# Four staging units of 12 KB, six output buffers and two turns of loads and stores in a batched matmul

## The chip, the cores and the metric

One core of one Trainium2 chip runs the kernel; the other cores are idle. The metric is the device time in microseconds of one execution. The 51 runs of the kernel before lie between 260.3 and 260.8 us (0.2%). A ratio is the mean time of one kernel's runs over the mean of the other's of the same rounds on the same chip, so it is not quite the ratio of the medians quoted beside it; the run that the profiler took stands among the times, but not in the ratio.

## The reference

```python
batch, m, k, n = 16, 512, 768, 1024
x: (16, 768, 512) float32      y: (16, 768, 1024) float32
out = np.einsum('bkm,bkn->bmn', x, y).astype(np.float32)
```

For each batch 1.57 MB of x and 3.15 MB of y are read and 2.10 MB of output is written: 75.5 MB in, 33.55 MB out.

## The kernel before

SyncE (SP) issues all transfers on one queue. VectorE (DVE) casts float32 to bfloat16, TensorE (PE) multiplies, ScalarE (ACT) copies PSUM to an output buffer. The parts that the change touches (cuts marked):

```python
x_v = x.rearrange("b (p ko) m -> b p ko m", ko=KT)     # KT = 6: a partition holds six rows of K,
y_v = y.rearrange("b (p ko) n -> b p ko n", ko=KT)     # x 12 KB, y 24 KB in one piece
FIRST = 8; TURN = 4; NO = 5
xs = [... sbuf_tensor(f"xs{i}", [P, KT, M], FP32) for i in range(2)]
ys = [... sbuf_tensor(f"ys{i}", [P, KT, N], FP32) for i in range(2)]
ob = [... sbuf_tensor(f"ob{i}", [P, MT, N], FP32) for i in range(NO)]
# ...
def load(b):
    i = b % 2
    if b >= 2:
        nc.sync.wait_ge(cast, nx[b - 2])                # x of b-2 is cast
    wide_dma("x", xs[i][:], x_v[b], 4, True).then_inc(sx[i], 16)
    if b >= 2:
        nc.sync.wait_ge(cast, nx[b - 2] + parts(b - 2)) # y of b-2 is cast
    wide_dma("y", ys[i][:], y_v[b], 2, True).then_inc(sy[i], 16)

for b in range(B):                                      # 8 loads, 4 stores, 4 loads, 4 stores, 4 loads
    load(b)
    if b + 1 >= FIRST and (b + 1 - FIRST) % TURN == 0:
        a = b + 1 - FIRST
        for c in range(a, a + TURN):
            store(c)                                    # waits until batch c + 1 is multiplied
for b in range(B - FIRST + TURN, B - 1):                # 7 stores; the last one follows at the very end
    store(b)
```

`wide_dma` describes a load so that the source is read in packets of 48 KB, four partitions of x or two of y (1440 packets of 49152 B in the trace); only the first load of each kind is described partition by partition (128 packets of 12288 B, 128 of 24576).

Of the kernel before, what the change touches and what calls it, by code (L numbers as in the profile page):

```python
# [3 lines left out]

# [2 lines left out]

# [7 lines left out]
@with_exitstack  # L15
def kernel(
    ctx: ExitStack,
    tc: tile.TileContext,
    x: bass.AP,
    y: bass.AP,  # L20
    out: bass.AP,
):
    nc = tc.nc
    P = 128
    FP32 = mybir.dt.float32
    BF16 = mybir.dt.bfloat16

    B, K, M = x.shape
    _, _, N = y.shape
    KT = K // P  # L30
    MT = M // P
    NF = 512
    NT = N // NF



    x_v = x.rearrange("b (p ko) m -> b p ko m", ko=KT)
    y_v = y.rearrange("b (p ko) n -> b p ko n", ko=KT)
    o_v = out.rearrange("b (p mo) n -> b p mo n", mo=MT)

    FIRST = 8
    TURN = 4
    NO = 5
    KH = KT // 2

    section = ExitStack()
    section.enter_context(tc.tile_critical())
    ec = ctx.enter_context
    xs = [ec(nc.sbuf_tensor(f"xs{i}", [P, KT, M], FP32)) for i in range(2)]
    ys = [ec(nc.sbuf_tensor(f"ys{i}", [P, KT, N], FP32)) for i in range(2)]  # L50
    xb = ec(nc.sbuf_tensor("xb", [P, 2, KT, M], BF16))
    yb = ec(nc.sbuf_tensor("yb", [P, 2, KT, N], BF16))
    ob = [ec(nc.sbuf_tensor(f"ob{i}", [P, MT, N], FP32)) for i in range(NO)]

    HB = MT // 2
    ps = [ec(nc.psum_tensor(f"ps{i}", [P, HB, NT, NF], FP32)) for i in range(2)]
    sx = [ec(nc.semaphore(f"sx{i}")) for i in range(2)]
    sy = [ec(nc.semaphore(f"sy{i}")) for i in range(2)]
    so = [ec(nc.semaphore(f"so{i}")) for i in range(NO)]
    cast = ec(nc.semaphore("cast"))  # L60
    ready = ec(nc.semaphore("ready"))
    room = ec(nc.semaphore("room"))
    groups = ec(nc.semaphore("groups"))
    idle = ec(nc.semaphore("idle"))
    outs = ec(nc.semaphore("outs"))


    made = {}

    def wide_dma(key, dst, src, dram_rows, load):  # L70


        if key not in made:
            made[key] = nc.sync.dma_start(dst, src)
            return made[key]
        pat = mybir.BassSymbolicTensorAccessPattern
        widen = lambda a: a.rearrange("(q r) k m -> q (r k m)", r=dram_rows)
        plain = lambda a: a.rearrange("p k m -> p (k m)")
        s, d = (widen(src), plain(dst)) if load else (plain(src), widen(dst))
        return nc.sync.add_instruction(_copy.replace(  # L80
            made[key].ins, name=nc.get_next_instruction_name(),
            ins=(pat(ap=s.ap, dtype=s.dtype, bass_ap=s, is_dma=False),),
            outs=(pat(ap=d.ap, dtype=d.dtype, bass_ap=d, is_dma=False),),
            sync_info=None, ant_dge_precooked=False))


    def parts(b):
        return 2 if b in (15,) else 1


    nx = [sum(1 + parts(a) for a in range(b)) + 1 for b in range(B)]



    def store(b):


        if b < B - 2:
            nc.sync.wait_ge(groups, 2 * (b + 2))
        else:  # L100
            nc.sync.wait_ge(outs, b - (B - 3))
        nc.sync.dma_start(o_v[b], ob[b % NO][:]).then_inc(so[b % NO], 16)

    def load(b):
        i = b % 2
        if b >= 2:
            nc.sync.wait_ge(cast, nx[b - 2])
        wide_dma("x", xs[i][:], x_v[b], 4, True).then_inc(sx[i], 16)
        if b >= 2:
            nc.sync.wait_ge(cast, nx[b - 2] + parts(b - 2))  # L110
        wide_dma("y", ys[i][:], y_v[b], 2, True).then_inc(sy[i], 16)

    for b in range(B):
        load(b)
        if b + 1 >= FIRST and (b + 1 - FIRST) % TURN == 0:
            a = b + 1 - FIRST
            for c in range(a, a + TURN):
                store(c)
    for b in range(B - FIRST + TURN, B - 1):
        store(b)  # L120


    for _ in range(60):
        nc.vector.sem_inc(idle, 1)
    for b in range(B):
        i = b % 2
        n = 16 * (b // 2 + 1)
        if b >= 2:
            nc.vector.wait_ge(groups, 2 * (b - 1))
        nc.vector.wait_ge(sx[i], n)  # L130
        nc.vector.tensor_copy(xb[:, i], xs[i][:]).then_inc(cast, 1)  # L131
        nc.vector.wait_ge(sy[i], n)
        for h in range(parts(b)):
            ks = slice(h * KT // parts(b), (h + 1) * KT // parts(b))
            nc.vector.tensor_copy(yb[:, i, ks], ys[i][:, ks]).then_inc(cast, 1)  # L135


    for b in range(B):
        nc.gpsimd.wait_ge(cast, nx[b]).then_inc(ready, 1)
        for h in range(parts(b)):  # L140
            nc.gpsimd.wait_ge(cast, nx[b] + h + 1).then_inc(ready, 2 // parts(b))


    x_w = xb[:].rearrange("p s k (j mo) -> p s k mo j", mo=MT)
    pe = OrderedEngineSet([nc.tensor.engine])
    with nc.Fori(0, B // 2, engines=pe):
        with nc.Fori(0, 2, engines=pe) as s:
            nc.tensor.wait_ge(ready, 2).then_inc(ready, -2)
            for mo in range(MT):
                g, m = divmod(mo, HB)  # L150
                if m == 0:
                    nc.tensor.wait_ge(room, 1).then_inc(room, -1)  # L152
                for kt in range(KT):
                    if mo == 0 and kt == KH:
                        nc.tensor.wait_ge(ready, 1).then_inc(ready, -1)
                    for nt in range(NT):
                        mm = nc.tensor.matmul(  # L157
                            ps[g][:, m, nt], x_w[:, bass.ds(s, 1), kt, mo],
                            yb[:, bass.ds(s, 1), kt, nt * NF:(nt + 1) * NF],
                            start=(kt == 0), stop=(kt == KT - 1))  # L160
                if m == HB - 1:
                    mm.then_inc(groups, 1)


    nc.scalar.nop().then_inc(room, 2)
    for _ in range(60):
        nc.scalar.sem_inc(idle, 1)
    for b in range(B):
        if b >= NO:
            nc.scalar.wait_ge(so[b % NO], 16 * (b // NO))  # L170
        for g in range(2):
            nc.scalar.wait_ge(groups, 2 * b + g + 1)
            cp = nc.scalar.copy(ob[b % NO][:, g * HB:(g + 1) * HB].rearrange("p m (t f) -> p m t f", f=NF),  # L173
                                ps[g][:])
            if b < B - 1:
                cp.then_inc(room, 1)
        if b == B - 2:
            nc.scalar.drain().then_inc(outs, 1)
    cp.then_inc(outs, 1)

    for b in range(B - NO, B - 2):
        nc.sync.wait_ge(so[b % NO], 16 * (b // NO + 1))
    section.close()




    nc.sync.dma_start(o_v[B - 1], ob[(B - 1) % NO][:])
# [30 lines left out]
```

## Time and profile before

| | before |
|---|---|
| time, median of 3 runs | 260.7 us (260.4 to 260.74) |
| span of the profile | 258.8 us |
| DMA queue, share of 16 engines | 98.6% |
| PE, DVE, ACT busy | 70%, 32%, 24% |
| transfers | 48 (16 of x, 16 of y, 16 of the output) |

The profile is to be read from the DMA row (the busy share of the sixteen DMA engines in 40 equal slices of the span, in tenths): it is at 8 or 9 in every slice but the first and the last, and every hole of PE lies over a full DMA row. The lines for that are in the prediction. The steady pace of the loads can be read from the casts of y in the timeline (start in us, duration, engine, line, what; in brackets the idle time before it and what ended it):

```profile
36.97 3.36 DVE L135 CAST yb<-ys 128x6144 bf16<-128x6144 f32 x1 [3.58 <-DMA ys<-in_y_dram]
47.97 3.36 DVE L135 CAST yb<-ys 128x6144 bf16<-128x6144 f32 x1 [4.23 <-DMA ys<-in_y_dram]
58.97 3.36 DVE L135 CAST yb<-ys 128x6144 bf16<-128x6144 f32 x1 [4.86 <-DMA ys<-in_y_dram]
```

A batch every 11.00 us, each cast waiting for its data. And the DMA part of the page has a second queue, which it names instruction:

```profile
q14 instruction: 2, 0.02, 0.0%
```

Two blocks of it within the span, at 9 and 11 us.

### The profile page before, as it was taken

The page shows a single profiled execution, that of the slowest core. Times are in us where ns is not written, and L with a number is a line of the kernel's source. Part 1 is how long each engine was busy: PE and PEld are TensorE (multiplying, and loading weights), DVE is VectorE, ACT ScalarE, POOL GpSimd, SP SyncE. Part 2 cuts the span into 40 slices and gives each one's busy share as a digit, 9 for nine tenths or more (in the row PEclk, how much of TensorE's full clock was granted, in tenths as well). Part 3 has the DMA queues.
Part 4 walks back from the last instruction along what each step waited for, and adds up shares of the span by engine and source line. Part 5 has one row for each costly group of instructions (what it writes and reads, how often), then busy time and mean ns, then how long its engine had stood idle before and what let it go on. Part 6 is the DMA issues. An engine that isn't in the chain of part 4 may idle for free. (4 is left out here: it accounts for less than half of the span.)

```text
span 258.8 us, 2506 instructions
## 1 busy us (share of the span) xinstructions
PE 181.6 (70%) x768; PEld 89.3 (34%) x768; DVE 82.0 (32%) x33; ACT 60.9 (24%) x33; POOL 0.2 (0%) x4
## 2 busy tenths in 40 slices
PE   0009999999999006999499920899669980099950
PEld 0004555554545002454145500355325530035520
DVE  0261645527164350011734525002255262300000
ACT  1000442234220005222214002324402200413430
POOL 0000000000000000000000000000000000000000
PEclk9999999999999855899779985699979995569995
DMA  7999989899999999999999989999899999999987
GB/s 273 424 475 410 471 380 479 372 479 395 456 410 441 387 418 430 466 446 418 433 433 425 471 352 443 420 461 479 372 479 403 448 410 390 433 438 420 436 357 324
DMA packets 4514, 109.07 MB, mean 421 GB/s; under 512 B 768, under 2 KB 768, under 8 KB 768
## 3 DMA queue, kind: packets, MB, share of 16 engines
q1 hardware_dynamic: 4512, 109.05, 98.6%
q14 instruction: 2, 0.02, 0.0%
HBM read 75.50 MB, written 33.55 MB: 421 GB/s over the span
## 5 line engine op out<-in xcount | busy, mean ns | idle before, releaser
L157 PE MATMUL ps<-yb,xb 128*128 x768 | 181.6, 402 | 68.0 <-PEq L152 68.0
L157 PEld LDWEIGHTS ps<-yb,xb 128*128 x768 | 89.3, 116 | 159.8 <-issue 89.8
L173 ACT COPY ob<-ps 128x2048 f32<-128x2048 f32 x32 | 59.6, 1872 | 185.3 <-PE ps L157 125.2
L135 DVE CAST yb<-ys 128x6144 bf16<-128x6144 f32 (+1 forms) x17 | 53.8, 3172 | 77.8 <-DMA ys<-in_y_dram 77.8
L131 DVE CAST xb<-xs 128x3072 bf16<-128x3072 f32 x16 | 28.2, 1761 | 62.5 <-DMA xs<-in_x_dram 48.7
L173 ACT ACT_TABLE_LOAD x1 | 1.3, 1283 | 5.3 <-issue 5.3
L203 POOL MEMSET const-bfloat16-1.0<- 128x1 bf16 x1 | 0.1, 103 | 0.0
L203 POOL MEMSET const-uint8-127<- 128x1 uint8 x1 | 0.1, 102 | 0.0
L203 POOL MEMSET const-float32-0.0<- 128x1 f32 x1 | 0.1, 100 | 0.2 <-issue 0.2
L203 POOL MEMSET const-float32-1.0<- 128x1 f32 x1 | 0.1, 99 | 0.0
## 6 DMA issues: line engine op xcount, KB each, us to landing
ys<-in_y_dram SPq DMA_DIRECT2D x16, 3072.0 KB, 18.6
out_dram<-ob SPq DMA_DIRECT2D x16, 2048.0 KB, 27.2
xs<-in_x_dram SPq DMA_DIRECT2D x16, 1536.0 KB, 20.1
```

What stands on the lines that cost most here:

```text
L131: nc.vector.tensor_copy(xb[:, i], xs[i][:]).then_inc(cast, 1)
L135: nc.vector.tensor_copy(yb[:, i, ks], ys[i][:, ks]).then_inc(cast, 1)
L157: mm = nc.tensor.matmul(ps[g][:, m, nt], x_w[:, bass.ds(s, 1), kt, mo], yb[:, bass.ds(s, 1), kt, nt * NF:(nt + 1) * NF], start=(kt == 0), ...
L173: cp = nc.scalar.copy(ob[b % NO][:, g * HB:(g + 1) * HB].rearrange("p m (t f) -> p m t f", f=NF), ps[g][:])
L203: nc = _bacc.Bacc("TRN2", target_bir_lowering=False, num_devices=1)
```

## The change

The intent: one more output buffer, so that the stores can be gathered in two stretches and the last output is ready before the stores ahead of it are done. The room for it comes from the staging: four units of 12 KB for each partition in place of two of x and two of y (48 KB in place of 72). A unit holds all of x of a batch, or half of y. The halves of y are halves of K, 384 rows each, three rows for each partition; x has to follow the same split, so its unit is filled by two loads. So a partition's piece in one load is 6 KB of x (was 12) and 12 KB of y (was 24), and a batch takes four loads (was two). A piece is what lies in one stretch in a partition; the prediction and the expectations call it a run.

```diff
-    x_v = x.rearrange("b (p ko) m -> b p ko m", ko=KT)
-    y_v = y.rearrange("b (p ko) n -> b p ko n", ko=KT)
+    x_v = x.rearrange("b (h p ko) m -> b h p ko m", h=2, ko=KH)
+    y_v = y.rearrange("b (h p ko) n -> b h p ko n", h=2, ko=KH)
-    FIRST = 8
-    TURN = 4
-    NO = 5
+    TURNS = [(9, 8), (7, 8)]
+    NO = 6
+    NU = 4
-    xs = [ec(nc.sbuf_tensor(f"xs{i}", [P, KT, M], FP32)) for i in range(2)]
-    ys = [ec(nc.sbuf_tensor(f"ys{i}", [P, KT, N], FP32)) for i in range(2)]
+    su = [ec(nc.sbuf_tensor(f"su{i}", [P, KT * M], FP32)) for i in range(NU)]
 ...
     def load(b):
-        i = b % 2
 ...
+        for u in range(3 * b, 3 * b + 3):
+            if u >= NU:
+                nc.sync.wait_ge(cast, u - NU + 1)
+            if u % 3 == 0:
+                st = su[u % NU][:].rearrange("p (h k m) -> p h k m", h=2, k=KH)
+                for h in range(2):
+                    wide_dma("x", st[:, h], x_v[b, h], 4, True).then_inc(sl[u % NU], 16)
+            else:
+                st = su[u % NU][:].rearrange("p (k n) -> p k n", k=KH)
+                wide_dma("y", st, y_v[b, u % 3 - 1], 4, True).then_inc(sl[u % NU], 16)
+
+    loads, stores = iter(range(B)), iter(range(B - 1))
+    for nl, ns in TURNS:
+        for b in islice(loads, nl):
+            load(b)
+        for b in islice(stores, ns):
+            store(b)
 ...  (the casts go by units, one for x and two for y; PE may start at the first half of y, before the change only in the last batch)
```

More of the change, by code (lines that the diff above doesn't have):

```diff
@@ L6 @@
 from contextlib import ExitStack
+from itertools import islice
 import concourse.bass as bass
@@ L33 @@
     NT = N // NF
-    x_v = x.rearrange("b (p ko) m -> b p ko m", ko=KT)
-    y_v = y.rearrange("b (p ko) n -> b p ko n", ko=KT)
+    KH = KT // 2
+    x_v = x.rearrange("b (h p ko) m -> b h p ko m", h=2, ko=KH)
+    y_v = y.rearrange("b (h p ko) n -> b h p ko n", h=2, ko=KH)
     o_v = out.rearrange("b (p mo) n -> b p mo n", mo=MT)
-    FIRST = 8
-    TURN = 4
-    NO = 5
-    KH = KT // 2
+    TURNS = [(9, 8), (7, 8)]
+    NO = 6
+    NU = 4
     section = ExitStack()
@@ L56 @@
     ps = [ec(nc.psum_tensor(f"ps{i}", [P, HB, NT, NF], FP32)) for i in range(2)]
-    sx = [ec(nc.semaphore(f"sx{i}")) for i in range(2)]
-    sy = [ec(nc.semaphore(f"sy{i}")) for i in range(2)]
+    sl = [ec(nc.semaphore(f"sl{i}")) for i in range(NU)]
     so = [ec(nc.semaphore(f"so{i}")) for i in range(NO)]
@@ L84, in wide_dma, with pieces, landed @@
             sync_info=None, ant_dge_precooked=False))
-    def parts(b):
-        return 2 if b in (15,) else 1
-    nx = [sum(1 + parts(a) for a in range(b)) + 1 for b in range(B)]
+    def pieces(u):
+        return 2 if u % 3 == 0 else 1
+    def landed(u):
+        return 16 * sum(pieces(v) for v in range(u % NU, u + 1, NU))
     def store(b):
@@ L104, in load @@
     def load(b):
-        i = b % 2
-        if b >= 2:
-            nc.sync.wait_ge(cast, nx[b - 2])
-        wide_dma("x", xs[i][:], x_v[b], 4, True).then_inc(sx[i], 16)
-        if b >= 2:
-            nc.sync.wait_ge(cast, nx[b - 2] + parts(b - 2))
-        wide_dma("y", ys[i][:], y_v[b], 2, True).then_inc(sy[i], 16)
-    for b in range(B):
-        load(b)
-        if b + 1 >= FIRST and (b + 1 - FIRST) % TURN == 0:
-            a = b + 1 - FIRST
-            for c in range(a, a + TURN):
-                store(c)
-    for b in range(B - FIRST + TURN, B - 1):
-        store(b)
+        for u in range(3 * b, 3 * b + 3):
[14 more added lines that the diff above has]
+            store(b)
     for _ in range(60):
@@ L125 @@
     for b in range(B):
-        i = b % 2
-        n = 16 * (b // 2 + 1)
         if b >= 2:
             nc.vector.wait_ge(groups, 2 * (b - 1))
-        nc.vector.wait_ge(sx[i], n)
-        nc.vector.tensor_copy(xb[:, i], xs[i][:]).then_inc(cast, 1)
-        nc.vector.wait_ge(sy[i], n)
-        for h in range(parts(b)):
-            ks = slice(h * KT // parts(b), (h + 1) * KT // parts(b))
-            nc.vector.tensor_copy(yb[:, i, ks], ys[i][:, ks]).then_inc(cast, 1)
-    for b in range(B):
-        nc.gpsimd.wait_ge(cast, nx[b]).then_inc(ready, 1)
-        for h in range(parts(b)):
-            nc.gpsimd.wait_ge(cast, nx[b] + h + 1).then_inc(ready, 2 // parts(b))
+        for u in range(3 * b, 3 * b + 3):
+            nc.vector.wait_ge(sl[u % NU], landed(u))
+            if u % 3 == 0:
+                to = xb[:, b % 2]
+            else:
+                h = u % 3 - 1
+                to = yb[:, b % 2, h * KH:(h + 1) * KH]
+            nc.vector.tensor_copy(to.rearrange("p k m -> p (k m)"), su[u % NU][:]).then_inc(cast, 1)
+    for u in range(3 * B):
+        nc.gpsimd.wait_ge(cast, u + 1).then_inc(ready, 1)
     x_w = xb[:].rearrange("p s k (j mo) -> p s k mo j", mo=MT)
```

## The prediction

Passages on the hardware that no trace or run of this case shows are cut from the prediction and from three of the expectations below, at the marks. The forecast's sum: 258.8 + 2.3 - 1.1 + 0.1 = 260.1 us of span, 262.0 of time. The 27.2 GB/s and 8 ns are a fit to the packets of one engine (12288 B in 460 ns, 16384 in 611, 24576 in 912); that the 8 ns go with each piece was the author's reading of them, an estimate.

> **What bounds the kernel now.** I read the page from the top: first which engine is full, then the slices, then the DMA rows, and only then the chain and the waits.
>
> ```profile
> span 258.8 us, 2506 instructions
> PE 181.6 (70%) x768; PEld 89.3 (34%) x768; DVE 82.0 (32%) x33; ACT 60.9 (24%) x33; POOL 0.2 (0%) x4
> PE   0009999999999006999499920899669980099950
> ...
> PEclk9999999999999855899779985699979995569995
> DMA  7999989899999999999999989999899999999987
> ...
> q1 hardware_dynamic: 4512, 109.05, 98.6%
> ...
> HBM read 75.50 MB, written 33.55 MB: 421 GB/s over the span
> ```
>
> No compute engine is above 70%, and PE has three holes (slices 14 to 15, 24 to 25, 34 to 35). The DMA row is at 8 or 9 in every slice but the first and the last, and the queue's packets fill 98.6% of the sixteen engines' span, through PE's holes too. So the transfers are the bound: 109 MB that have to move whatever the order. The chain of waits shows only the last 13% of the span, so it does not contradict this; it shows the one place where compute does set the end:
>
> ```profile
> 225.71 0.27 issue
> 225.98 23.61 PE ps L157 x96
> 249.59 0.02 issue
> 249.61 1.87 ACT ob L173
> ```
>
> The last 96 matmuls start at 226 because ScalarE got an output buffer only then; the last copy ends at 251.5 and the last store is issued at 251.67. By that time the stores before it are done. The three holes are the same wait, for a buffer still being stored. The view of waits (total us, times, longest):
>
> ```profile
> PE ps L157 <- PEq L152: 68.0, 8, 18.9
> ACT ob L173 <- DMA out_dram<-ob: 60.1, 3, 21.7
> ```
>
> and the first hole and the last issue in the timeline (start, duration):
>
> ```profile
> 97.00 3.64 ACT L173 COPY ob<-ps 128x2048 f32<-128x2048 f32 x2 [21.69 <-DMA out_dram<-ob]
> 99.19 23.85 PE L157 MATMUL ps<-yb,xb 128*128 x96 [14.79 <-PEq L152]
> ...
> 251.67 0.33 SPq L188 DMA_DIRECT2D out_dram<-ob  x1
> ```
>
> They look costly, 60 us in all, but the DMA row has no hole beside them, so removing one is worth nothing by itself.
>
> **Where the DMA's time goes.** I followed the packet records of one of the 16 DMA engines through the trace. First packet at 1.97 us; eight batches of loads until 90.83 (88.86 us); four stores (19.46); four batches of loads, 110.29 to 154.12 (43.83); four stores (19.45); four batches (43.86); seven stores until 251.46 (34.04); nothing for 1.11; the last store, 4.92, until 257.49; then 1.31 to the end. Loads 176.55, stores 77.87, and 4.39 idle: 258.81. At each change of direction the next packet starts in the same 10 ns as the last one ends, so a turn has no visible cost. That leaves little: 1.97 and 1.31 are start and completion, and only 1.11 is a real hole.
>
> What does a packet cost? Median by size: 12288 B 460 ns, 16384 B 611, 24576 B 912. These fit 8 ns plus bytes at 27.2 GB/s (451.8 + 8, 602.4 + 8, 903.5 + 8). The 49152 B packets of the loads take 1815 ns just after a turn (1807 + 8), but in a steady stretch x packets take 1842 and 1848 and y packets 1825 to 1829. A 48 KB packet of x is four partitions of 12 KB, one of y two of 24 KB: 4 x 460 = 1840 and 2 x 912 = 1824. So I read it so: [...] 8 ns for each run in a partition. For one engine and batch: 294912 B / 27.2 = 10.842 us, 16 runs x 8 ns = 0.128, and two 4-byte semaphore packets of 9 ns = 0.018, together 10.988. The casts of y in the first stretch are 11.0 apart (36.97, 47.97, 58.97), so the sum closes.
>
> [...] PEclk falls to 5 after each hole, and 96 matmuls take 22.9 to 23.9 us after one, against 20.7 for two batches in the warm stretch (10.36 each).
>
> **The change, part by part.**
> 1. Two turns in place of three. Worth about 0, from the packet records above.
> 2. Runs of half the length. x now comes in two loads of 6 KB for each partition, y in two of 12 KB. For one engine and batch the runs go from 8 + 8 to 16 + 16: 16 x 8 ns = 0.128 us more. Loads go from two to four, so two more semaphore packets: 0.018. Together 0.146 us for each batch, 10.988 to 11.134, and times 16 it is 2.3 us, all on the bound. (The sum of bytes is the same.)
> 3. The end. The last eight stores are now in one queue. Call its first store packet T. ScalarE gets a buffer when the first of them has landed: 97.00 - 90.35 (first store packet) = 6.65 after T; PE starts 2.19 later; PE needs a batch, 10.4 + 3.2 cold = 13.6, then the last copy: about T + 24.5. The DMA is busy with seven stores until T + 34. SP waits for the store of batch 13, landed about T + 31, then issues the last one, whose first packet follows 0.9 after its issue (251.67 to 252.57): T + 32.5. So the hole of 1.11 goes.
> 4. First store phase. Stores 0 to 5 are issued at once. Store 7 waits for batch 8 to be multiplied, and batches 7 and 8 can only start when store 0 has landed: T + 6.65 + 2.19 + 23.85 = T + 32.7, first packet T + 33.6; the first engine runs dry at 7 x 4.864 = T + 34.05. It fits by 0.4 us (by 1.4 with the 22.86 of the second hole). I put 0.1 for a bubble. The loads after it find their units free (cast since about T + 4) and follow at once.
> 5. Load phases. A unit is refilled when it is cast; the queue then holds three units, 3 x 3.7 = 11 us. Landing (1.5), cast (1.76) and issue (1.4) take under 5, so the queue does not run dry. DVE casts y as two of 1.76 in place of one of 3.36, 0.16 more in each batch, hidden (DVE is at 32%). PE starts a batch at its first half of y, earlier than now; hidden.
> Sum: 258.8 + 2.3 - 1.1 + 0.1 = 260.1 of span. By stretches: 1.97 + (9 x 11.134 + 0.96, the start's extra seen before: 88.86 - 8 x 10.988) = 103.1; + 38.9 = 142.1; + 7 x 11.134 = 220.0; + 38.9 + 1.3 = 260.2. The timed median is 1.9 above the profile's span (260.7 against 258.8): 262.0.
>
> **Rivals.**
> First, runs cost nothing and only the tail's hole counts: 258.8 - 1.1 + 0.3 for the extra semaphores = 258.0 of span, timed 259.9. For it: the 1815 ns packets after a turn. Against: they rise to 1842 in every later batch.
> Second, fewer turns buy much[...]: then below 257. Against: gapless packets at every turn, and with all bytes at the best packet rates the sum is 252.6 us plus start and end, 255.9; a gain of 2% (span 253.6) lies below that floor.
> Third, store 7 comes late, since its margin is 0.4 us: if PE is held at a low clock for longer, or a copy is late, each microsecond beyond goes straight into the time. Two us of it make 264; 2% would need over 5, which no hole seen here suggests (22.9, 23.9 and 23.6 us for the same 96 matmuls).
> Fourth, smaller loads and a longer run of loads leave the queue short because of a cast held up by PE. PE is done with a batch about 12.3 us after its data are in, and the cast that needs it is ready 16 after; 4 us of slack and 11 of queue speak against it.
>
> **Range and chances.** The middle is the sum, 261.9. If runs cost half of what I think, 260.8; with none, 259.9; with a bubble of 1.5 us, 263.4. I take 260.2 to 263.4. Faster by over 2% (below 255.5) is under the floor: 0.01. Slower by over 2% (above 265.9) needs a bubble of 4 us: 0.03. The rest, 0.96, is within 2%.
>
> **What would show it.** Packets of y at about 1842 to 1850 ns in place of 1829, packets of x (24 KB) at about 936 in place of 912; first store packet at about 102.6; ScalarE waiting twice in place of three times for a store, until about 109 and 226; the last store with no hole before it. Wrong if 48 KB packets of y stay at 1829, if the DMA row shows a dip near slices 21 to 22 (end of the first store phase), or if the hole before the last store is still there.

## The result, and the profile after

The changed kernel takes 264.3 us (median of 4 runs, 264.09 to 264.59) against 260.6 (4 runs, 260.4 to 260.74); ratio 1.0143, 95% interval 1.0126 to 1.0161. That is slower beyond noise, and above the predicted range of 260.2 to 263.4. The page:

```profile
span 262.1 us, 2568 instructions
...
PE   0059999999999940089970049999999999099000
...
DMA  6999999999999998999999999999999999999996
...
q1 hardware_dynamic: 5568, 109.06, 98.6%
q14 instruction: 3, 0.02, 0.0%
HBM read 75.50 MB, written 33.55 MB: 416 GB/s over the span
```

The DMA row is as full as before, with no dip at slices 21 and 22 (the last packets of the first store phase were slow all the same, see step 4 below), and yet the same bytes move at 416 in place of 421 GB/s: the full queue has become slower. Note 5568 packets in place of 4512, and three blocks of instructions in place of two. The chain of work that ended last:

```profile
4 pieces in order of time: start us, us, what
229.14 0.22 issue
229.36 12.51 PE ps L154 x48
241.87 0.02 issue
241.89 1.87 ACT ob L170
```

The last copy ends at 243.8, 7.7 us sooner than the 251.5 of the kernel before, although the program ends 3.3 later. The waits (total us, times, longest) and the timeline show the two long waits for a stored buffer, at the places predicted (until 109 and 226 there, 110.45 and 227.17 here), and the last store issued long before it can start:

```profile
ACT ob L170 <- DMA out_dram<-ob: 38.8, 2, 25.0
```

```profile
110.45 3.64 ACT L170 COPY ob<-ps 128x2048 f32<-128x2048 f32 x2 [24.99 <-DMA out_dram<-ob]
112.64 23.19 PE L154 MATMUL ps<-yb,xb 128*128 x96 [17.95 <-PEq L149]
...
227.17 3.64 ACT L170 COPY ob<-ps 128x2048 f32<-128x2048 f32 x2 [13.86 <-DMA out_dram<-ob]
229.36 12.49 PE L154 MATMUL ps<-yb,xb 128*128 x48 [6.82 <-PEq L149]
...
252.18 0.33 SPq L185 DMA_DIRECT2D out_dram<-ob  x1
```

So everything that the change meant to do for the engines happened. The loads' pace, from the casts of the second half of y:

```profile
38.72 1.76 DVE L134 CAST yb<-su 128x3072 bf16<-128x3072 f32 x1 [1.92 <-DMA su<-in_y_dram]
...
49.87 1.76 DVE L134 CAST yb<-su 128x3072 bf16<-128x3072 f32 x1 [1.93 <-DMA su<-in_y_dram]
```

11.15 us for a batch, in place of 11.00. The packets are as the prediction said: in the steady stretch a 48 KB packet of y takes 1848 ns in the median (1842 to 1850 foretold, 1829 before) and a 24 KB packet of x 939 (936 foretold); the first store packet starts at 102.97 us (102.6 foretold). To see more, one has to go to the packet records. Every transfer leaves a 4-byte semaphore packet on each of the 16 engines (768 packets for 48 transfers, 1280 for 80); the records carry no engine number, but these packets come in groups of sixteen, so one can tell when a transfer is done on the fastest engine, on average, and on the slowest (where two groups overlap at the start, to some tenths of a us):

| us | before: mean, slowest | changed: mean, slowest |
|---|---|---|
| batch 0 loaded | 13.85, 14.50 | 14.86, 15.85 |
| one batch, mean over batches 1 to 7 | 10.994 | 11.131 |
| last store but one done | 251.53, 252.46 | 255.02, 255.97 |
| first packet of the last store | 252.50 | 254.74 |
| last store done | 257.49, 257.57 | 259.88, 260.83 |
| span | 258.81 | 262.10 |

Read the slowest engine: it is the one that ends the program. It is 1.35 us later after the first batch; from there to the end it takes 244.98 in place of 243.07, 1.91 more. Fifteen batches at 0.137 are 2.06. And the hole before the last store: in the kernel before the slowest engine finishes its part at 252.46 and the last store starts at 252.50. It had no hole. The hole of 1.11 us, which the prediction had found by following one engine, belonged to an engine that was ahead.

### The profile page after: what moved, and what is told of

The parts are those of the page before. It is cut to its first block, busy times and chain, and to the rows that moved or that the text cites. A ratio compares the mean times of both kernels' runs of the same rounds, so it can differ in the third digit from the quotient of the medians.

```text
span 262.1 us, 2568 instructions
## 1 busy us (share of the span) xinstructions
PE 177.3 (68%) x768; PEld 88.3 (34%) x768; DVE 84.5 (32%) x48; ACT 60.9 (23%) x33; POOL 0.2 (0%) x4
## 2 busy tenths in 40 slices
DMA packets 5571, 109.08 MB, mean 416 GB/s; under 512 B 1280, under 2 KB 1280, under 8 KB 1408
## 3 DMA queue, kind: packets, MB, share of 16 engines
q1 hardware_dynamic: 5568, 109.06, 98.6%
## 5 line engine op out<-in xcount | busy, mean ns | idle before, releaser
L154 PE MATMUL ps<-yb,xb 128*128 x768 | 177.3, 393 | 64.5 <-PEq L149 58.1
L154 PEld LDWEIGHTS ps<-yb,xb 128*128 x768 | 88.3, 115 | 153.0 <-issue 82.1
L134 DVE CAST yb<-su 128x3072 bf16<-128x3072 f32 x32 | 56.3, 1760 | 60.7 <-DMA su<-in_y_dram 60.7
L134 DVE CAST xb<-su 128x3072 bf16<-128x3072 f32 x16 | 28.2, 1760 | 78.9 <-DMA su<-in_x_dram 78.9
```

The source lines that it names most:

```text
L134: nc.vector.tensor_copy(to.rearrange("p k m -> p (k m)"), su[u % NU][:]).then_inc(cast, 1)
L154: mm = nc.tensor.matmul(ps[g][:, m, nt], x_w[:, bass.ds(s, 1), kt, mo], yb[:, bass.ds(s, 1), kt, nt * NF:(nt + 1) * NF], start=(kt == 0), ...
```

## The experiments

In the labels b_ is an edit of the kernel before, a_ one of the changed kernel. Batch 0 (when it is loaded, us) and the pace of a batch are means over the 16 engines, from the profiled run; the pace is that of batches 1 to 7 (b_early and b_late: 2 to 7).

| run | time, us (lowest to highest) | ratio to before (95%) | batch 0 | a batch |
|---|---|---|---|---|
| b_halves | 263.47 (263.37 to 264.5) | 1.0116 (1.0100 to 1.0131) | 14.54 | 11.131 |
| b_runs | 273.43 (273.34 to 273.47) | 1.0490 (1.0474 to 1.0506) | 14.87 | 11.745 |
| b_turns | 260.49 (260.24 to 260.69) | 0.9992 (0.9979 to 1.0006) | 14.09 | 10.980 |
| a_turns3 | 263.59 (263.41 to 263.98) | 1.0117 (1.0101 to 1.0132) | 13.77 | 11.132 |
| a_same | 263.87 (263.23 to 265.38) | 1.0117 (1.0100 to 1.0134) | 14.43 | 11.130 |
| a_yfirst | 263.72 (263.64 to 263.79) | 1.0118 (1.0103 to 1.0134) | 14.00 | 11.143 |
| a_x1 | 263.5 (263.27 to 263.68) | 1.0112 (1.0096 to 1.0127) | 14.07 | 11.140 |
| a_12k | 262.38 (261.95 to 262.58) | 1.0067 (1.0053 to 1.0081) | 14.24 | 11.085 |
| a_97 | 263.86 (263.69 to 264.14) | 1.0127 (1.0112 to 1.0143) | 13.87 | 11.138 |
| a_delay | 263.72 (263.23 to 263.99) | 1.0123 (1.0107 to 1.0138) | 13.73 | 11.132 |
| a_start2 | 263.73 (263.65 to 263.79) | 1.0120 (1.0105 to 1.0136) | 14.06 | 11.141 |
| b_turns97 | 260.71 (260.67 to 260.77) | 1.0003 (0.9990 to 1.0017) | 14.07 | 10.979 |
| b_early | 261.07 (260.69 to 261.96) | 1.0024 (1.0011 to 1.0037) | 13.79 | 11.011 |
| b_late | 263.46 (263.21 to 263.59) | 1.0110 (1.0096 to 1.0125) | 14.05 | 11.141 |
| b_pad | 261.41 (261.14 to 261.5) | 1.0027 (1.0014 to 1.0041) | 14.10 | 10.984 |

All are correct. The kernel before took 260.57 to 260.72 (medians) beside them.

**b_halves: half loads alone, in the kernel before.**

```diff
-        wide_dma("x", xs[i][:], x_v[b], 4, True).then_inc(sx[i], 16)
+        for h in range(2):
+            wide_dma("x", xs[i][:, h * KH:(h + 1) * KH], x_v[b, h], 4, True).then_inc(sx[i], 16)
-        wide_dma("y", ys[i][:], y_v[b], 2, True).then_inc(sy[i], 16)
+        for h in range(2):
+            wide_dma("y", ys[i][:, h * KH:(h + 1) * KH], y_v[b, h], 4, True).then_inc(sy[i], 16)
```

> The kernel before, with each load of x and y cut into the two half loads of the change (runs of 6 and 12 KB in a partition in place of 12 and 24), and nothing else: same staging, buffers and order. Theory (runs cost 8 ns each[...], plus a slow start with more and smaller first loads): each batch of loads takes 11.13 us on one DMA engine in place of 10.99, so +2.3 us, and about +1 us at the start: about 264 us, ratio 1.011 to 1.014. Rival (the loss comes from the four units, the six buffers or the order of loads and stores): within 0.5 us of the kernel before.

Ratio 1.0116, and in its timeline the casts of y, still whole, come 11.13 apart:

```profile
38.56 3.36 DVE L137 CAST yb<-ys 128x6144 bf16<-128x6144 f32 x1 [3.26 <-DMA ys<-in_y_dram]
49.69 3.36 DVE L137 CAST yb<-ys 128x6144 bf16<-128x6144 f32 x1 [4.04 <-DMA ys<-in_y_dram]
```

This one edit alone brings most of the loss, without units, buffers or turns. The rival that blamed those for it is out.

**b_runs: shorter pieces, the same number of loads.**

```diff
-    x_v = x.rearrange("b (p ko) m -> b p ko m", ko=KT)
-    y_v = y.rearrange("b (p ko) n -> b p ko n", ko=KT)
+    x_v = x.rearrange("b (ko p) m -> b p ko m", ko=KT)
+    y_v = y.rearrange("b (ko p) n -> b p ko n", ko=KT)
-        wide_dma("x", ...)   and   wide_dma("y", ...)
+        nc.sync.dma_start(xs[i][:], x_v[b])   and   nc.sync.dma_start(ys[i][:], y_v[b])
```

> The kernel before with the same number of loads, but each partition's part of a load in six runs (x 2 KB, y 4 KB), from another split of K over the partitions. A dose test of the 8 ns per run: 96 runs for one engine and batch in place of 16, 80 x 8 ns = 0.64 us per batch, 16 batches 10.2 us: about 271 us, ratio 1.039. If the number of loads and their semaphores is what costs, and not the runs, it stays at the kernel before. If a run costs only what bytes cost, likewise.

273.43 us, ratio 1.049: more than the 1.039 expected. The batch went to 11.745, 0.751 above the kernel before for 80 more pieces on an engine: 9.4 ns each, where 8 were assumed. The timeline:

```profile
28.14 3.36 DVE L135 CAST yb<-ys 128x6144 bf16<-128x6144 f32 x1 [5.92 <-DMA ys<-in_y_dram]
39.89 3.36 DVE L135 CAST yb<-ys 128x6144 bf16<-128x6144 f32 x1 [4.79 <-DMA ys<-in_y_dram]
51.63 3.36 DVE L135 CAST yb<-ys 128x6144 bf16<-128x6144 f32 x1 [5.85 <-DMA ys<-in_y_dram]
```

So here shorter pieces cost 0.751 us a batch at an unchanged number of loads. In this run the reading side is cut into pieces of 2 and 4 KB as well (27392 packets on the page in place of 4512), so the run does not say which of the two costs.

**b_turns: six buffers and two turns alone, in the kernel before.**

```diff
-    FIRST = 8
-    TURN = 4
-    NO = 5
+    TURNS = [(9, 8), (7, 8)]
+    NO = 6
 ...  (the order of loads and stores as in the change)
```

> The kernel before with the six buffers and the two turns of the change alone (its own loads and staging kept). The prediction's step 3 says that the hole of 1.11 us before the last store goes: 259.5. My theory now: the slowest DMA engine had no hole (its last packet before it ended at 252.46, the last store began at 252.57), so the gain is 0.1 to 0.3 us: 260.3 to 260.5. If two turns in place of three were the harm of the change, it would be slower than before, by 2 us or more.

260.49 us, ratio 0.9992 with an interval that holds 1. The profile's chain, last store and span:

```profile
239.23 0.02 issue
239.25 1.87 ACT ob L170
```

```profile
248.89 0.33 SPq L185 DMA_DIRECT2D out_dram<-ob  x1
```

```profile
span 258.8 us, 2506 instructions
```

ACT is done at 241.1 in place of 251.5 and the last store is issued at 248.89 in place of 251.67, and the span is the same 258.8. On the fastest engine the last transfer ends at 256.42 in place of 257.44, on the slowest at 257.56 in place of 257.57. That is step 3 of the prediction, measured by itself: worth 0.2 us at most. Two turns do no harm either.

**a_turns3: three turns in the changed kernel.**

```diff
-    TURNS = [(9, 8), (7, 8)]
+    TURNS = [(8, 4), (4, 4), (4, 7)]
```

> The changed kernel with the order of the kernel before (8 loads, 4 stores, 4 loads, 4 stores, 4 loads, 8 stores), six buffers and four units kept. Theory (turns cost nothing): within 0.3 us of the changed kernel, about 264.3. Rival (the longer stretches of one direction harm): back towards 261.

1.0117, as the unedited kernel on its second chip (1.0117, below): turns are worth nothing, as step 1 said. It is 0.7 us below the first result of the changed kernel, more than expected, and its profile shows where: batch 0 is there at 13.77 in place of 14.86 us, although up to that point the two kernels are the same. The start varies from run to run, or from chip to chip.

**a_same: the changed kernel again, no edit.**

> The changed kernel once more, unedited, for runs on one chip with the next three and for a second profile of its start. In the run with the old order of turns the first batch landed (mean of the 16 DMA engines) at 13.8 us, in the first profile of the changed kernel at 14.9, with the same instructions up to there. If the start is a matter of the run or the chip, this run's start lies somewhere between 13.8 and 14.9 and the time between 263.4 and 264.6; if it belongs to the kernel, 14.9 and 264.3 again.

Four runs from 263.23 to 265.38. The start lay between the two, at 14.43. With the first four runs that is a scatter of 2.1 us in eight runs, against 0.24 in the nine runs of the kernel before beside them. The profiled run was the slowest one (265.38); its slowest engine ends 1.95 us behind the mean. The ratio of 1.0117 leaves that run out.

**a_yfirst, a_start2, a_delay: other starts.** Batch 0 alone: half of y first; half of y first and x as one load; the next batch's x held back.

```diff
-        for u in range(3 * b, 3 * b + 3):
+        for u in (1, 0, 2) if b == 0 else range(3 * b, 3 * b + 3):      # a_yfirst and a_start2
```

```diff
+                if b == 0:                                              # a_start2 also
+                    nc.sync.dma_start(st, x_v[b].rearrange("h p k m -> p h k m")).then_inc(sl[u % NU], 16)
```

```diff
+            if u == 3:                                                  # a_delay
+                nc.sync.wait_ge(sl[0], 32)
```

> The changed kernel with the first half of y issued ahead of the two halves of x, in batch 0 only. Theory[...]: the first load is now 1.57 MB, the engines start closer together, batch 0 lands 0.5 to 1 us earlier, and the time falls by as much: 263.3 to 263.8. Rival (the start costs the same whatever comes first[...]): no change against the unedited kernel of the same call.

> The changed kernel with batch 0 started differently: first half of y first, then x in one load in place of two. If the small first loads are what delays and scatters the start, batch 0 lands at about 13.9 us on average (13.85 in the kernel before, 14.0 with y first alone), and the time is 263.3 to 263.7, with runs within 0.3 us of each other where the unedited kernel's lie 2.1 apart. If not, 264.2 and as scattered.

> The changed kernel with the two x loads of batch 1 held back until batch 0's x has landed, so that four loads in place of six are issued at the start. If the late and scattered start comes from too many loads issued at once[...], batch 0 lands at 13.8 to 14.2 us on average of the engines in place of 14.4 to 14.9, and the time is about 263.5 with less scatter. If it comes from the small first loads themselves, no change: 14.4 to 14.9 and 264.2.

Medians of 263.72, 263.73 and 263.72, starts of 14.00, 14.06 and 13.73. The first two have very close runs, within 0.15 us, where the unedited ones lie 2.1 apart. That fits the theory, but the unedited start was also seen at 13.77 and 13.87, and the ratio does not move (1.0118 to 1.0123 against 1.0117): no edit of the start buys time that the runs can tell from nothing. Why the start scatters is open.

**a_x1: one load of x in place of two, pieces still 6 KB.**

```diff
-                for h in range(2):
-                    wide_dma("x", st[:, h], x_v[b, h], 4, True).then_inc(sl[u % NU], 16)
+                nc.sync.dma_start(st, x_v[b].rearrange("h p k m -> p h k m")).then_inc(sl[u % NU], 16)
```

> The changed kernel with each batch's x in one load in place of two; the runs in a partition stay at 6 KB. If runs set the pace and the number of loads costs only a 9 ns semaphore packet, the steady batch falls by 0.01 to 0.02 us (0.2 us in all), and the start may gain up to 1 us as there are fewer and larger first loads: 263.2 to 264.2. If the number of loads is what costs (rival), a third of the 2.3 us comes back: below 263.5 with a steady batch of 11.08.

1.0112 and a batch of 11.140: taking sixteen loads out does not make the pace better. The rival (the number of loads costs) asked for 11.08. The run settles a second rival, which nobody had named: that the packets in which the source is read cost, and not the pieces written. Without `wide_dma` x is read in packets of 6 KB in place of 24, and the page counts 8288 packets in place of 5568,

```profile
q1 hardware_dynamic: 8288, 109.06, 99.0%
```

in the steady stretch twelve more for an engine and a batch, with the same pieces and within 0.01 us the same pace. At 8 ns each they would have cost 0.1.

**a_12k: pieces of 12 KB for x and y.**

```diff
-    x_v = x.rearrange("b (h p ko) m -> b h p ko m", h=2, ko=KH)
-    y_v = y.rearrange("b (h p ko) n -> b h p ko n", h=2, ko=KH)
+    x_v = x.rearrange("b (p ko) m -> b p ko m", ko=KT)
+    y_v = y.rearrange("b (p h ko) n -> b h p ko n", h=2, ko=KH)
 ...  (x in one load; each half of y takes three of a partition's six rows)
```

> The changed kernel with x in one load whose runs are 12 KB again, and y in two loads with runs of 12 KB as in the change (the K rows of a partition lie together as in the kernel before, and a half of y takes three of its six rows). Eight runs fewer for one engine and batch: 64 ns, and one load fewer: 9 ns; 16 x 0.073 = 1.2 us less: steady batch 11.06, time 262.5 to 263.2. If run lengths do not matter, no change.

262.38, ratio 1.0067, 1.5 us below the unedited kernel; a batch of 11.085, where 11.06 was expected. So x's pieces of 12 KB, with the load that goes and the fetch that goes with it (see b_pad), give back over a third of the loss. a_x1 has the same number of loads, the same order and no such fetch either, and stays 1.1 us above it: that is the pieces, 0.9 of it by the pace (16 x 0.055). (The halves of y are described partition by partition here, so the source is read in more packets than in the changed kernel, 7776 on the page in place of 5568, and the batch is shorter all the same: again it is not the reading packets that cost.)

**a_97: no store issued late.**

```diff
-    TURNS = [(9, 8), (7, 8)]
+    TURNS = [(9, 7), (7, 8)]
```

> The changed kernel with 7 stores in the first turn in place of 8 (9 loads, 7 stores, 7 loads, 8 and the last stores). In both profiles of the changed kernel the last packets of the eighth store took up to 1.29 us in place of 0.61 (near 141 us), because that store can be issued only when batch 8 is multiplied, just as the queue runs out. With it moved to the last stretch, no such packets: 0.2 to 0.6 us less than the unedited kernel (264.2 over its 8 runs). If the slow packets are a cost of every change of direction and not of the late issue, they appear after the seventh store as well, and the time stays.

The slow store packets near 141 us are gone (three load packets at 139.4 are slow in their place), but the time is 263.86, ratio 1.0127: no gain. A miss: these packets cost mostly engines that are ahead.

**b_turns97: the same order in the kernel before, as a candidate to beat both.**

> The kernel before with six buffers and the order 9 loads, 7 stores, 7 loads, 9 stores: a version that should beat both. The hole before the last store is filled and no store is issued late: 260.2 to 260.6, at most 0.2% faster than the kernel before. If it is faster than that by 1 us, the prediction's step 3 was right after all and the eighth store's late issue hid it in the other run.

260.71, ratio 1.0003. The kernel before stays the best to within the noise.

**b_early and b_late: half loads in batches 0 and 1 only, or in batches 2 to 15 only.** The edit is that of b_halves under `if b < 2:` or `if b >= 2:`.

> The kernel before with half loads in batches 0 and 1 only. The runs of two batches are worth 2 x 0.14 = 0.3 us; all beyond it is the start. If the start belongs to the half loads: 261.2 to 262.0, with runs scattered by up to 1 us, and batch 0 landing at 13.8 to 14.9 on average of the engines. If the start costs nothing and the whole loss is in the steady stretch: 260.9.

> The kernel before with half loads in batches 2 to 15 only; its start is that of the kernel before. Theory: 14 x 0.14 = 1.9 us: 262.4 to 262.7, runs as close together as those of the kernel before, batch 0 at 13.85. The two runs' losses should add up to that of the run with all loads halved (2.8 to 3.1 us). If this one alone reaches 263.4, the start is no separate term.

b_early: 261.07, runs from 260.69 to 261.96, ratio 1.0024. Of its 0.4 us two batches at 0.137 explain 0.27, so the start costs 0.15 in the median and 1 us in the worst run: a small term with a long tail, smaller than I had put it. b_late: 263.46, 2.8 us above the kernel before, more than the 1.9 that I had expected of 14 batches; the runs are close together. A miss that led on: in its profile the slowest engine falls from 0.79 to 1.45 us behind the mean between two stores, and at that place an instruction block of 8192 B (0.318 us, at 247.29) stands between packets, the next of which takes 892 ns in place of 611.

**b_pad: the instruction fetch by itself.** The kernel before with a longer program on SP, in a place where SP waits anyway:

```diff
         load(b)
+        if b == 1:
+            for _ in range(60):
+                nc.sync.sem_inc(idle, 1)
```

> The kernel before with 60 idle semaphore increments in SP's program after the first two batches of loads, where SP waits anyway. In every profile of a kernel with 76 or more transfers the queue that fetches instructions reads one more 8 KB block in mid-run (at 210 to 247 us; 0.31 us, and the packet behind it takes 0.40 longer on that one DMA engine); kernels with 64 or fewer have none. If it is the length of SP's program, the padding brings such a fetch here too. Its cost is then 0 where it falls on a fast engine (the kernel before has up to 1 us of slack there, ahead of its last store) and up to 0.7 where it falls on the slowest: 260.6 to 261.3. If no fetch appears, SP's length is not the cause.

261.41, all five runs between 261.14 and 261.5, ratio 1.0027. The page has a third block:

```profile
q1 hardware_dynamic: 4512, 109.05, 98.4%
q14 instruction: 3, 0.02, 0.0%
```

It comes at 70.39 us and takes 0.309; the load packet behind it takes 2.251 in place of 1.83. So a program on SP that is 60 instructions longer, with the same transfers, cost 0.7 us here (261.41 against 260.72). (Its next load is issued at 9.46 in place of 8.97 us; the queue is full then.) How the 0.7 us reach the end: in this profile the slowest engine was no later than before by batch 7. But the packets of the engine with the fetch can be followed, each starting within 4 ns of the end of the one before (some starts fit two engines, so the path is likely, not certain). It is 0.26 us behind the mean of the sixteen just after the fetch, falls back further in each stretch of stores, with many packets at 0.62 to 0.65 us, is the slowest from 111 us on, and is 1.75 us behind when the last store begins. Why a late engine's store packets take longer is open.

Such an extra block within the span is in the changed kernel (at 215.28, the load packet behind it 2.253) and in every edit with 76 transfers or more, and in none with 64 or fewer, but for b_pad. What it does there can be read from the lag of the slowest engine behind the mean just before and just after it: 1.04 to 1.59 us in a_same, 0.67 to 1.22 in a_turns3, 0.56 to 1.22 in a_yfirst, 0.59 to 1.07 in a_start2, 0.74 to 1.05 in a_97, 0.79 to 1.45 in b_late, but nothing in the first profile (0.93 to 0.87), in a_delay (1.03 to 0.98) and in b_halves (1.29 to 1.26). In the runs without such a block the lag does not move at that place (0.78 in a_x1, 0.62 in a_12k, 0.45 in b_turns). So the block sets the slowest engine back by 0.3 to 0.7 us there, or not at all. That this depends on which engine it falls on, as the expectation of b_pad has it, fits, but is not shown. Yet a_x1, without the block, is only 0.1 to 0.3 us faster by ratio than the unedited kernel and the three edits of its start (1.0112 against 1.0117 to 1.0123), so for the changed kernel's time 0.7 is too much.

## Why the prediction was wrong

The direction, the main cause (shorter pieces) and the class (within 2%) were right; the time was 2.0 us too low in the span (260.1 against 262.1), so the range missed it.

- Step 1, turns cost nothing: right (a_turns3, b_turns), and with it the second rival is out.
- Step 2, pieces of half the length, 0.146 us a batch: right, and the first rival (pieces cost nothing) is out. 0.137 measured in the changed kernel and the same in b_halves; 16 x 0.137 = 2.2 us of 2.3. Dose (b_runs, 9.4 ns a piece) and partial reversal (a_12k, 5.8) agree in kind with the change's 8.6 (0.137 us for 16), semaphore packets included; a piece has no fixed price. That the packets of the reading side do not set this price is shown by a_x1 (8288 packets in place of 5568, a batch of 11.140 in place of 11.131) and a_12k (7776, 11.085); what does set it was not shown.
- Step 3, "So the hole of 1.11 goes": this is the term that failed. It was measured on one engine of sixteen and taken for all. For the slowest engine the hole was 0.04 us (252.46 to 252.50), and filling it by itself gains 0.2 us at most (b_turns). About 1 us of the miss.
- Step 4, store 7 fits by 0.4 us: nearly. It was issued 32.9 us after the first store packet, as reckoned (32.7); its last packets took up to 0.7 us longer, mostly on engines that were ahead (a_97: no gain). The margin of 0.4 counts the 0.9 us from issue to first packet that the last store showed (251.67 to 252.57 in the profile before). The third rival, several us of bubble, is out.
- Step 5, the queue does not run dry: right; the DMA row shows it.
- Three terms were missing. The start: the prediction took over the 0.96 us of the kernel before. With half loads it scatters; the slowest engine was 1.2 us later in the first profile (1.35 less 0.14 for the pieces), while b_early puts it at 0.15 in the median and 1 in the worst case. The instruction fetch, which the longer program of SP brings about: 0.7 us in b_pad, and between nothing and 0.7 with 80 transfers. And 0.2 us outside the profile's span: the time is 1.74 to 1.83 us above the span in every run of the b_ edits, whatever their loads and turns, and 1.95 to 2.05 in every run of the changed kernel and its edits; the prediction added 1.9. What in the changed kernel does this no run shows.

For b_halves the terms add up: pieces 2.2 + fetch 0.7 + start 0.15 = 3.05 against 3.0 (1.16% of 260.7). But the fetch and the start are taken from other runs, and in the profile of b_halves the fetch did not set the slowest engine back, so this is a fit and not a measurement. For the changed kernel the same sum, with 0.2 outside the span and up to 0.2 less for the hole, is again about 3.1, against 3.1 on the second chip (1.17%) and 3.7 in the first four runs (1.43%). In the first profile the fetch does not show as a further lag of the slowest engine (0.93 us behind the mean before it, 0.95 at the end), and the late start does: 1.1 for the hole and 1.2 for the start, less 0.1 for the bubble that was added and 0.1 for the pieces, which came out smaller, are 2.1 against the 2.0 that were missing. So how the last 1 to 1.5 us divide between start and fetch differs from run to run, and the scatter of the start itself is not explained.

## What to carry to other kernels

The queue of this kernel was full (98.6% of its engines' span), and of the 3.1 to 3.7 us that the change cost 2.2 came from the pieces and semaphore packets that it added to that queue (16 x 0.137). Count the contiguous pieces in a partition before cutting a load in two to save a buffer; here 16 more a batch on each engine cost 0.85% and the engines' better order gained nothing. And take a hole in a queue from the slowest of its engines, not from the one that was easiest to follow: the sixteen ended the last store 0.13 us apart before the change and 1.69 after it, and the 1.11 us that one of them waited was slack (filling it gained 0.2 us at most, b_turns).
